# The two float32r parts of a stationary weight in one buffer, element by element, in a decoder trunk on one Trainium2 core

## Chip, cores and metric

One core of one Trainium2 chip runs the whole program in a single launch. The metric is the device time of that launch in microseconds (us). Three runs of the kernel before gave 2358.15, 2359.06 and 2359.34 us; the median, 2359.06 us, is what the change is held against.

## What is computed

Two layers of a decoder trunk on x of 512 tokens by 1024 channels, in float32, and a last RMSNorm. Each layer has two sub-layers:

```
h = rmsnorm(x, norm1_w)
(z, xbc, dt, gq, gk, gv, g_lr, g_r, qkv, gates) = split(h @ w_in)       # 1024 -> 12320 columns
y_ssd, y_gla, y_att = state space, gated linear attention, dilated window attention
merged = sum_i sigmoid(gates_i) * (y_i @ w_branch_i)
x = x + merged @ w_out
h = rmsnorm(x, norm2_w)
gate, val = split(h @ ffn_up)                                           # 1024 -> 2 x 2816
x = x + (silu(causal_conv3(gate)) * val) @ ffn_down
```

Nearly all of the arithmetic is in the products with w_in, w_branch, w_out, ffn_up and ffn_down.

## The kernel before

**How a product is made.** Each float32 operand is split in two float32r parts, a high part h and a rest lo, so that h + lo is the value. A product is then three matmuls into the same PSUM bank (`mm3`): high with high, high with rest, rest with high. The activations of a layer lie in eight pairs of tiles `xh`, `xl` of 128 channels by 512 tokens, written once per norm. The weights come in units of 128 x 1024 values. There are 374 of them, in the order of `weight_plan`, and each takes 24 matmuls of 512 columns.

**A weight unit.** `unit` (it takes unit u) calls `fetch(u + 6)`, which issues the transfer of a unit from HBM into one of four `raw` buffers on SyncE's queue, and `parts(u + 3)`, which splits a unit: ScalarE copies `raw` into the float32r tile `wh` (line 248) and VectorE subtracts that from `raw` into `wl` (line 250). The pool `wgt` has three buffers of each.

**Two kinds of unit.** In a unit "cm" (`proj_cm`, `branch` and the down projection; 318 units) the weights are stationary: TensorE loads 128 columns of `wh` or `wl` and streams 512 columns of an activation pair past them. The activation is `xh`/`xl` in 226 units (113 a layer) and a pair from the pool `big` in 92: `ya`, `yg`, `ys` (branch outputs), `mg` (merged), `hh`/`hl` (hidden layer of the MLP). In a unit "tm" (`proj_tm`; 56 units) it is the other way round: 128 columns of `xh` or `xl` are loaded, and 512 columns of `wh` or `wl` stream. In 40 of these the loaded columns lie side by side (`blk`), in 16 they are read with a step of four elements (`res`).

**Order of work.** TensorE runs its matmuls in the order in which the code records them. The large matmuls of a unit wait in a queue, `large`; the small float32 matmuls of the side work (scores, scans, transposes) are recorded between units, and each is followed by one large matmul (line 182; the others are on line 177). The instructions of VectorE and ScalarE are ordered by the framework's scheduler.

**Where buffers lie.** Pools are laid out in the order in which they are opened. In the built program `xh` and `xl` (pool `cp`) fill bytes 30688 to 63455 of each partition, `wh` and `wl` bytes 86720 to 111295, `big` bytes 111296 to 217791. 30688 is 32 more than a multiple of 64; 86720 and 111296 are multiples of 64, and every tile of these pools is a multiple of 2048 bytes long, so that all of a pool's tiles share that remainder. `own_c`, a small stationary operand of the state space branch, starts at 28128, which also is 32 more than a multiple of 64.

Of the kernel before, what the change touches and what calls it, by code (L numbers as in the profile page):

```python
# [12 lines left out]
F32R = mybir.dt.float32r  # L13
# [5 lines left out]
PSUM = bass.MemoryType.PSUM  # L19

P = 128
T = 512
D = 1024
KD = D // P
# [7 lines left out]

# columns of the packed per-channel parameters
O_N1, O_N2, O_SCW, O_SCB, O_SNW, O_GB, O_GNW, O_FCW, O_FCB, N_PC = (
    0, 8, 16, 80, 96, 104, 106, 107, 173, 195)


# The order of the work between the projections of the linear attention and the gates of the state
# space branch: z (two groups), x/B/C of a group, two output blocks of the other branches.
MIX = ([("att", m) for m in (0, 2, 4, 6)] + [("z", 0), ("xbc", 0), ("xbc", 1), ("gla", 0), ("z", 1), ("xbc", 2)]  # L40
# [3 lines left out]
def weight_plan(depth):  # L44
    """The order in which the kernel takes its weight units (128 x 1024 values each)."""
    plan = []
    for l in range(depth):
# [23 lines left out]
        for kind, n in MIX:  # L71
# [5 lines left out]
            else:  # L77
                i, row = (2, 12) if kind == "att" else (1, 8)
# [18 lines left out]
def shape_constants():  # L97
    """Arrays that depend on the shapes alone."""
    f = np.float32
# [37 lines left out]
def hybrid_decoder(ctx: ExitStack, tc: tile.TileContext, ins, out):  # L137
    nc = tc.nc
    depth = ins["pc"].shape[0]
    plan = weight_plan(depth)  # L140
# [3 lines left out]
    def nm(s):  # L144
        ids[0] += 1
        return f"{s}_{ids[0]}"

    cp = ctx.enter_context(tc.tile_pool(name="cp", bufs=1))
    lp = ctx.enter_context(tc.tile_pool(name="lp", bufs=1))
    raw_p = ctx.enter_context(tc.tile_pool(name="raw", bufs=4))  # L150
    wgt_p = ctx.enter_context(tc.tile_pool(name="wgt", bufs=3))
    big_p = ctx.enter_context(tc.tile_pool(name="big", bufs=52))
    sml_p = ctx.enter_context(tc.tile_pool(name="sml", bufs=20))
# [15 lines left out]

    # The large matmuls of a weight unit wait in a queue, and each small one of the side work is  # L170
    # followed by one of them: a small one's stationary operand then loads behind a large one.
    large = deque()
# [26 lines left out]

    # ---- side work: generators that are stepped between weight units; each yields the number of  # L200
    # units after which the operands of its next step are there ----
    sides = []
# [31 lines left out]

# [1 line left out]
    raws, units = [], []  # L236
# [7 lines left out]
    def parts(n):  # L244
        while len(units) < min(n, len(plan)):
            r = raws[len(units)]
            h = wgt_p.tile([P, 1024], F32R, tag="wh", name=nm("wh"))
            A.copy(h, r)  # L248
            lo = wgt_p.tile([P, 1024], F32R, tag="wl", name=nm("wl"))
            V.tensor_sub(lo, r, f(h))  # L250
            units.append((h, lo))
# [39 lines left out]

# [1 line left out]
    mats = cp.tile([P, 3, P], F32, name="mats")  # L293
# [5 lines left out]
    pcs, rows, gws = [], [], []  # L299
# [24 lines left out]

    xh = [cp.tile([P, T], F32R, name=f"xh{m}") for m in range(KD)]
    xl = [cp.tile([P, T], F32R, name=f"xl{m}") for m in range(KD)]
    xhl = list(zip(xh, xl))
    rstdB = cp.tile([P, T], F32, name="rstdB")
# [15 lines left out]

# [1 line left out]
    def split(h, lo, src, w):  # L346
        """h + lo = src * w"""
        A.activation(h, src, AF.Copy, scale=w)  # L348
        V.scalar_tensor_tensor(lo, src, w, f(h), ALU.mult, ALU.subtract)
# [12 lines left out]
    def norm_stats(acc, both):  # L362
        """rstdB, and the factors of the tokens in block (and residue) order"""
        n = 8 if both else 4
        ss = mx()
        for c in range(n):
            mm(ss[:, c:c + 1], acc[:, blk(c) if c < 4 else res(c - 4)], ones[:, 0:1], True, True)
        return factors(ss, n)
# [18 lines left out]

# [1 line left out]
    def attention(yh, yl, pre):  # L389
# [36 lines left out]
    def attention_head(h, vt, qk, yh, yl):  # L426
        hc = blk(h)
        # scores, masked, with their row maxima: [0] block order, [1] residue order
        st = [sml([P, 2, 4], n="st") for _ in range(2)]
        pr = []  # L430
        for d in range(2):
            for half in range(2):
                s = mx()
                for j in range(2):
                    n = 2 * half + j
                    if d == 0:
                        lo = 0 if n else P
# [6 lines left out]
                p = big([P, 2, 256], n="pr")  # L444
                for j in range(2):
                    n = 2 * half + j
                    lo = P if (d == 0 and n == 0) else 0
# [3 lines left out]
        for d in range(2):  # L451
            nb = sml([P, 4], n="nb")
            V.tensor_scalar(nb, st[d][:, 0], -ATT_C, None, ALU.mult)
            for n in range(4):
                lo = P if (d == 0 and n == 0) else 0
                p = pr[2 * d + n // 2][:, n % 2, lo:]
                A.activation(p, p, AF.Exp, bias=nb[:, n:n + 1], scale=ATT_C, accum_out=st[d][:, 1, n:n + 1])
        # the groups' weights: exp(m - M) / sum, computed in residue order
        ex = sml([P, 4, 2, 4], n="ex")
# [34 lines left out]
        for d in range(2):  # L494
            for n in range(4):
                lo = P if (d == 0 and n == 0) else 0
# [3 lines left out]
        yield 1  # L500
        # transposes; block-order columns go to (residue, index) order
        pt = []
# [29 lines left out]

# [1 line left out]
    def small_proj():  # L534
# [5 lines left out]

# [1 line left out]
    def gla_decay(l, gd, las):  # L542
# [147 lines left out]

# [1 line left out]
    def ssd_decay(l, gd, dec):  # L692
# [14 lines left out]
        A.activation(u, u, AF.Exp)  # L707
        # log1p(u) = 2 atanh(z), z = u / (2 + u) <= 1/3
        rd = sml([P, n], n="rd")
# [25 lines left out]
        V.tensor_mul(dte, dt, e[:, 1])  # L735
        # the cumulative sums as rows (twice): the upper copy is replaced by the rest of the split
        ac2 = big([P, 2, 64], n="ac2")
# [16 lines left out]
    def conv_silu(o, width, w, b, dst):  # L754
        """dst = 2 w-conv of (o * rstd), then v (tanh v + 1): w and b are halved"""
        x = big([P, T], n="cx")
        V.tensor_mul(x, o, rstdB)  # L757
        v = big([P, T], n="cv")
        A.activation(v, x, AF.Identity, bias=b, scale=w(width - 1))
        for i in range(1, width):  # L760
            V.scalar_tensor_tensor(v[:, i:], x[:, :T - i], w(width - 1 - i), v[:, i:], ALU.mult, ALU.add)  # L761

        def end():
            A.activation(x, v, AF.Tanh)  # L764
            V.scalar_tensor_tensor(dst, x, 1.0, v, ALU.add, ALU.mult)

        return end
# [25 lines left out]
    def ssd_group(l, g, dec, ch, zw, yh, yl):  # L793
# [10 lines left out]

        # token-major x and B
        xdt, xd, xe = [], [], []
# [91 lines left out]

# [1 line left out]
    def gate():  # L900
# [41 lines left out]

# [1 line left out]
    def new_acc():  # L944
# [18 lines left out]
    for l in range(depth):  # L963
# [76 lines left out]
        if not end:  # L1040
            side(norm_side(acc, True), 2)
# [1 line left out]
    sq = big([P, T], n="sq")  # L1043
# [16 lines left out]
def lay_out(inputs):  # L1060
    """The program's arrays: the inputs, rearranged only."""
    a = {k: np.asarray(v) for k, v in inputs.items()}
# [54 lines left out]
```

## Time and profile before

| | us |
|---|---|
| median of three runs | 2359.06 |
| span of the profiled execution | 2355.0 |
| difference, outside the span | 4.1 |
| TensorE matmul busy (10776 instructions) | 2332.6 (99%) |
| TensorE weight load busy | 1921.1 (82%) |
| VectorE busy | 1413.3 (60%) |
| ScalarE busy | 902.9 (38%) |
| DMA queue 1, share of 16 engines | 27.9% |

How to read it: the profile is of one execution, whose span is 4.1 us under the median of the runs; what a step saves of the span it saves of the median. Matmuls are pipelined, so that a record of a matmul is longer than the time from its start to the next one's start; it is the latter that adds up to the span, and the timeline's start times give it. A weight load (PEld) runs beside the matmul before it. "Idle before" is time in which an engine waited, with the instruction that ended the wait.

### The profile page before, as it was taken

Reading aid. Unit: us, or ns where it says so; the run is one execution under the profiler, and the core shown is the slowest. Engines: PE = TensorE matmul, PEld = TensorE weight load, DVE = VectorE, ACT = ScalarE, POOL = GpSimd, SP = SyncE. Lnnn points to the kernel's source line nnn. Section 1 sums busy time; section 2 is a strip of 40 time slices with the busy share of each in tenths; the row PEclk is TensorE's granted clock in tenths of the full one; section 3 lists DMA queues with packets and bytes.
Section 4 is the critical chain, followed back from the end, with each engine's and each line's share of the span. In section 5 each row is a group of like instructions: output and inputs, shape, how many; then the busy total and the mean of one; then the engine's idle time right before and its main releaser. Section 6 shows DMA issues by size and latency. Waiting matters only on the chain.

```text
span 2355.0 us, 27385 instructions
## 1 busy us (share of the span) xinstructions
PE 2332.6 (99%) x10776; PEld 1921.1 (82%) x10776; DVE 1413.3 (60%) x2511; ACT 902.9 (38%) x1487; POOL 0.2 (0%) x4
## 2 busy tenths in 40 slices
PE   8999999999999999999999999999999999999997
PEld 7888878888888888888898888788888888888886
DVE  4467548687865565553425764676888556555533
ACT  4344423444443333332224444234454433333321
POOL 0000000000000000000000000000000000000000
PEclk9999999999999999999999999999999999999998
DMA  5322222222222323233323222222222232333231
GB/s 180 99 81 78 75 63 90 79 65 72 81 81 90 99 90 99 90 99 94 95 89 99 81 81 70 73 82 72 72 74 79 81 99 90 99 90 99 91 98 54
DMA packets 58512, 204.21 MB, mean 87 GB/s; under 512 B 7152, under 2 KB 7824, under 8 KB 58384
## 3 DMA queue, kind: packets, MB, share of 16 engines
q1 hardware_dynamic: 57808, 201.42, 27.9%
q8 instruction: 84, 1.38, 0.2%
q10 hardware_dynamic: 576, 1.05, 0.1%
q14 instruction: 44, 0.36, 0.0%
HBM read 200.35 MB, written 2.10 MB: 86 GB/s over the span
## 4 chain that ended last, share of the span: by engine, by line
PE 98%; DVE 1%; ACT 0%; DMA 0%; issue 0%; DVEq 0%; SPq 0%; ACTq 0%
PE pp L177 78%; PE pp L182 11%; PE mx L185 8%; PE mx L189 1%; DVE x L1055 0%; DVE wl L250 0%; DMA x<-in_xT 0%; ACT wh L248 0%; DVE th L904 0%; DVE th L929 0%; DVE cv L761 0%; ACT L348 0%; ACT cx L764 0%; ACT th L905 0%; DVE M L882 0%
## 5 line engine op out<-in xcount | busy, mean ns | idle before, releaser
L248 ACT CAST wh<-raw 128x1024 fp32r<-128x1024 f32 x374 | 392.3, 1049 | 992.1 <-PE pp L177 764.0
L250 DVE TENSOR_TENSOR wl<-raw,wh 128x1024 fp32r<-128x1024 f32 x374 | 457.7, 1224 | 374.5 <-ACT wh L248 368.9
L177 PE MATMUL pp<-xh,wl 128*128 128x512 f32 x1582 | 625.2, 395 | 0.0
L177 PE MATMUL pp<-xl,wh 128*128 128x512 f32 x1556 | 614.9, 395 | 0.0
L177 PE MATMUL pp<-xh,wh 128*128 128x512 f32 x1504 | 595.0, 396 | 0.0
L177 PEld LDWEIGHTS pp<-xh,wl 128*128 128x128 f32 x1582 | 297.0, 188 | 72.1 <-issue 1.0
L177 PEld LDWEIGHTS pp<-xl,wh 128*128 128x128 f32 x1556 | 292.3, 188 | 68.9 <-issue 0.5
L177 PEld LDWEIGHTS pp<-xh,wh 128*128 128x128 f32 x1504 | 282.4, 188 | 68.8 <-DVE wl L250 1.5
L177 PE MATMUL pp<-wh,xl 128*128 128x512 f32 x392 | 156.1, 398 | 0.0
L177 PE MATMUL pp<-wh,xh 128*128 128x512 f32 x372 | 148.4, 399 | 7.3 <-ACT wh L248 7.3
L177 PE MATMUL pp<-wl,xh 128*128 128x512 f32 x386 | 154.6, 401 | 0.5 <-DVE wl L250 0.5
L182 PE MATMUL pp<-xh,wh 128*128 128x512 f32 x304 | 148.1, 487 | 0.0
L177 PE MATMUL pp<-hh,wh 128*128 128x512 f32 x352 | 137.1, 390 | 0.0
L177 PE MATMUL pp<-hh,wl 128*128 128x512 f32 x352 | 137.1, 390 | 0.0
L177 PE MATMUL pp<-hl,wh 128*128 128x512 f32 x352 | 137.1, 389 | 0.0
L757 DVE TENSOR_TENSOR cx<-pp,rstdB 128x512 f32<-128x512 f32 x76 | 52.4, 689 | 129.7 <-PE pp L177 129.6
L182 PE MATMUL pp<-xl,wh 128*128 128x512 f32 x252 | 124.4, 494 | 0.0
L182 PE MATMUL pp<-xh,wl 128*128 128x512 f32 x226 | 110.4, 489 | 0.0
L764 ACT ACTIVATE cx<-cv 128x512 f32<-128x512 f32 x76 | 48.1, 632 | 138.7 <-DVE cv L761 138.2
L177 PEld LDWEIGHTS pp<-wh,xh 128*128 128x128 f32 x372 | 86.2, 232 | 18.3 <-ACT wh L248 7.3
L177 PEld LDWEIGHTS pp<-wh,xl 128*128 128x128 f32 x392 | 89.9, 229 | 11.7
L177 PEld LDWEIGHTS pp<-wl,xh 128*128 128x128 f32 x386 | 88.8, 230 | 12.5 <-DVE wl L250 1.0
(267 smaller groups left out, 3389.4 us busy)
## 6 DMA issues: line engine op xcount, KB each, us to landing
raw<-in_wall SPq DMA_DIRECT2D x374, 512.0 KB, 3.6
x<-in_xT SPq DMA_DIRECT2D x8, 256.0 KB, 5.9
out_dram<-x ACTq DMA_DIRECT2D x4, 256.0 KB, 2.3
out_dram<-x SPq DMA_DIRECT2D x4, 256.0 KB, 2.5
cosR<-in_rope SPq DMA_DIRECT2D x2, 256.0 KB, 3.9
sinR<-in_rope SPq DMA_DIRECT2D x2, 256.0 KB, 4.7
amask<-in_amask SPq DMA_DIRECT2D x1, 256.0 KB, 5.3
levf<-in_lev SPq DMA_DIRECT2D x1, 224.0 KB, 3.6
```

Of the source, the lines that this page charges most:

```text
L177: PE.matmul(o, lhsT=l, rhs=r, start=start, stop=stop)
L182: PE.matmul(o, lhsT=l, rhs=r, start=start, stop=stop)
L185: PE.matmul(o, lhsT=l, rhs=r, start=start, stop=stop)
L189: PE.transpose(o, i, idn)
L248: A.copy(h, r)
L250: V.tensor_sub(lo, r, f(h))
L757: V.tensor_mul(x, o, rstdB)
L764: A.activation(x, v, AF.Tanh)
```

## The change

`wh` and `wl` of a unit become one tile `w` of 2048 elements. In a unit "cm" the high part takes the even elements and the rest the odd ones, so that the load of 128 stationary columns reads every second element. In a unit "tm" the two parts lie one behind the other and stream as before. ScalarE's copy and VectorE's subtraction write, and VectorE reads the high part, with a step of two in units "cm". Two pools are opened in another order, and `xh`, `xl` get a pool of their own (the diff's lines that only drop comments are left out):

```diff
     cp = ctx.enter_context(tc.tile_pool(name="cp", bufs=1))
     lp = ctx.enter_context(tc.tile_pool(name="lp", bufs=1))
+    xp = ctx.enter_context(tc.tile_pool(name="xp", bufs=1))
     raw_p = ctx.enter_context(tc.tile_pool(name="raw", bufs=4))
+    big_p = ctx.enter_context(tc.tile_pool(name="big", bufs=52))
     wgt_p = ctx.enter_context(tc.tile_pool(name="wgt", bufs=3))
-    big_p = ctx.enter_context(tc.tile_pool(name="big", bufs=52))
...
             r = raws[len(units)]
-            h = wgt_p.tile([P, 1024], F32R, tag="wh", name=nm("wh"))
+            w = wgt_p.tile([P, 2048], F32R, tag="w", name=nm("w"))
+            if plan[len(units)][0] == "tm":
+                h, lo = w[:, :1024], w[:, 1024:]
+            else:
+                wv = w.rearrange("p (n two) -> p two n", two=2)
+                h, lo = wv[:, 0], wv[:, 1]
             A.copy(h, r)
-            lo = wgt_p.tile([P, 1024], F32R, tag="wl", name=nm("wl"))
             V.tensor_sub(lo, r, f(h))
             units.append((h, lo))
...
-    xh = [cp.tile([P, T], F32R, name=f"xh{m}") for m in range(KD)]
-    xl = [cp.tile([P, T], F32R, name=f"xl{m}") for m in range(KD)]
+    xh = [xp.tile([P, T], F32R, name=f"xh{m}") for m in range(KD)]
+    xl = [xp.tile([P, T], F32R, name=f"xl{m}") for m in range(KD)]
```

In the built program of the change `xh` and `xl` fill bytes 37568 to 70335, `big` bytes 86720 to 193215 and `w` bytes 193216 to 217791; 37568 and 193216 are multiples of 64, as 86720 is. `own_c` stays where it was. The number and the order of TensorE's matmuls and of SyncE's transfers are the same; the scheduler moves the split of a unit on ScalarE and VectorE, as follows.

ScalarE, in the projections of the first attention head of layer 0 (`sw` are the halves of a rotated product, copied out of PSUM `pp`; `raw`, `wh` and `w` belong to the split). Before:

```order
L248 CAST wh_658<-raw_551 128x1024
L248 CAST wh_697<-raw_581 128x1024
L413 COPY sw_686<-pp_655 64x512
L414 COPY sw_686<-pp_655 64x512
L248 CAST wh_736<-raw_611 128x1024
L413 COPY sw_725<-pp_694 64x512
L414 COPY sw_725<-pp_694 64x512
```

And with the change:

```order
L254 CAST w_647<-raw_543 128x1024
L418 COPY sw_674<-pp_644 64x512
L419 COPY sw_674<-pp_644 64x512
L254 CAST w_685<-raw_572 128x1024
L418 COPY sw_712<-pp_682 64x512
L419 COPY sw_712<-pp_682 64x512
L254 CAST w_723<-raw_601 128x1024
```

The copy of a unit's high part stood ahead of the two copies out of PSUM of the same step; now it stands behind them.

VectorE at the same place (`ra`, `sw` and `qk` are the rotation of a product). Before:

```order
L250 TENSOR_TENSOR wl_699<-raw_581,wh_697 128x1024
L416 TENSOR_TENSOR ra_689<-pp_655,cosR_649 128x512
L417 TENSOR_TENSOR sw_686<-sw_686,sinR_650 128x512
L422 TENSOR_TENSOR qk_692<-ra_689,sw_686 128x512
L250 TENSOR_TENSOR wl_738<-raw_611,wh_736 128x1024
L416 TENSOR_TENSOR ra_728<-pp_694,cosR_649 128x512
```

And with the change:

```order
L421 TENSOR_TENSOR ra_677<-pp_644,cosR_638 128x512
L422 TENSOR_TENSOR sw_674<-sw_674,sinR_639 128x512
L255 TENSOR_TENSOR w_685<-raw_572,w_685 128x1024
L427 TENSOR_TENSOR qk_680<-ra_677,sw_674 128x512
L421 TENSOR_TENSOR ra_715<-pp_682,cosR_638 128x512
L422 TENSOR_TENSOR sw_712<-sw_712,sinR_639 128x512
```

The subtraction stood ahead of the rotation of the same step; now it stands behind the rotation's first two instructions.

## Rows read from the trace of the kernel before

**Rows 1.** The page: busy time of the engines, and the granted TensorE clock in 40 slices of the span (tenths; 9 is 90% or more).

```profile
PE 2332.6 (99%) x10776; PEld 1921.1 (82%) x10776; DVE 1413.3 (60%) x2511; ACT 902.9 (38%) x1487; POOL 0.2 (0%) x4
...
PEclk9999999999999999999999999999999999999998
```

**Rows 2.** The page: the chain of work that ended last, shares of the span by engine and by line.

```profile
PE 98%; DVE 1%; ACT 0%; DMA 0%; issue 0%; DVEq 0%; SPq 0%; ACTq 0%
PE pp L177 78%; PE pp L182 11%; PE mx L185 8%; PE mx L189 1%; DVE x L1055 0%; DVE wl L250 0%; DMA x<-in_xT 0%; ACT wh L248 0%; DVE th L904 0%; DVE th L929 0%; DVE cv L761 0%; ACT L348 0%; ACT cx L764 0%; ACT th L905 0%; DVE M L882 0%
```

**Rows 3.** TensorE's waits on the split: who waited for whom, us in total, how often, the longest.

```profile
PE pp L177 <- ACT wh L248: 7.3, 1, 7.3
...
PE pp L177 <- DVE wl L250: 0.5, 1, 0.5
```

**Rows 4.** Groups of TensorE's matmuls by line and shape: out<-moving,stationary, partitions x columns, count | busy us, mean ns of one record | idle before.

```profile
L177 PE MATMUL pp<-xh,wl 128*128 128x512 f32 x1582 | 625.2, 395 | 0.0
...
L177 PE MATMUL pp<-wh,xl 128*128 128x512 f32 x392 | 156.1, 398 | 0.0
...
L182 PE MATMUL pp<-xh,wh 128*128 128x512 f32 x304 | 148.1, 487 | 0.0
L177 PE MATMUL pp<-hh,wh 128*128 128x512 f32 x352 | 137.1, 390 | 0.0
...
L177 PE MATMUL pp<-ysh,wh 128*128 128x512 f32 x128 | 49.9, 390 | 0.0
...
L177 PE MATMUL pp<-mgh,wh 128*128 128x512 f32 x128 | 49.8, 389 | 0.0
...
L177 PE MATMUL pp<-yah,wl 128*128 128x512 f32 x56 | 21.9, 391 | 0.0
...
L185 PE MATMUL mx<-qsb,ksb 128*128 128x128 f32 x224 | 42.9, 273 | 0.0
...
L185 PE MATMUL mx<-xg,own_c 128*128 128x512 f32 x32 | 12.6, 395 | 0.0
...
L185 PE MATMUL mx<-qsb,ksb 128*128 128x512 f32 x16 | 8.2, 591 | 0.0
```

**Rows 5.** Groups of TensorE's weight loads, same columns.

```profile
L177 PEld LDWEIGHTS pp<-xh,wl 128*128 128x128 f32 x1582 | 297.0, 188 | 72.1 <-issue 1.0
...
L177 PEld LDWEIGHTS pp<-hl,wh 128*128 128x128 f32 x352 | 66.1, 188 | 13.6
```

**Rows 6.** Timeline of TensorE in the up projection of the MLP of layer 0 (units "cm", moving `xh`/`xl`): start us, duration us, engine, line. First and last of 26 matmuls in a row.

```profile
902.78 0.40 PE L177 MATMUL pp<-xl,wh 128*128 128x512 f32 x1
...
908.61 0.39 PE L177 MATMUL pp<-xh,wl 128*128 128x512 f32 x1
```

**Rows 7.** The same in the down projection of layer 0 (units "cm", moving `hh`/`hl`): first and last of 26.

```profile
1099.80 0.39 PE L177 MATMUL pp<-hh,wl 128*128 128x512 f32 x1
...
1105.46 0.39 PE L177 MATMUL pp<-hh,wh 128*128 128x512 f32 x1
```

**Rows 8.** The same in a unit "tm" whose stationary columns lie side by side: first and last of 27, and one load.

```profile
19.66 0.40 PE L177 MATMUL pp<-wh,xh 128*128 128x512 f32 x1
...
19.89 0.19 PEld L177 LDWEIGHTS pp<-wh,xl 128*128 128x128 f32 x1
...
25.73 0.40 PE L177 MATMUL pp<-wh,xl 128*128 128x512 f32 x1
```

**Rows 9.** The same in a unit "tm" whose stationary columns are read with a step of four elements: first and last of 28, and one load.

```profile
39.42 0.40 PE L177 MATMUL pp<-wh,xl 128*128 128x512 f32 x1
...
40.14 0.31 PEld L177 LDWEIGHTS pp<-wh,xh 128*128 128x128 f32 x1
...
45.84 0.40 PE L177 MATMUL pp<-wh,xl 128*128 128x512 f32 x1
```

**Rows 10.** Groups of ScalarE and VectorE. The outputs of lines 530 and 531 are written with a step of four elements; those of lines 248, 250, 1014 and 416 without a step.

```profile
L248 ACT CAST wh<-raw 128x1024 fp32r<-128x1024 f32 x374 | 392.3, 1049 | 992.1 <-PE pp L177 764.0 <-issue 201.6 <-PE pp L182 20.4
...
L1014 ACT CAST hh<-fs 128x512 fp32r<-128x512 f32 x44 | 27.3, 621 | 4.3 <-DVE fs L1012 4.2
...
L530 ACT CAST yah<-mx 128x512 fp32r<-128x512 f32 x8 | 8.6, 1079 | 40.8 <-PE mx L185 40.8
...
L250 DVE TENSOR_TENSOR wl<-raw,wh 128x1024 fp32r<-128x1024 f32 x374 | 457.7, 1224 | 374.5 <-ACT wh L248 368.9 <-PE mx L185 4.0
...
L416 DVE TENSOR_TENSOR ra<-pp,cosR 128x512 f32<-128x512 f32 x48 | 33.1, 689 | 17.1 <-ACT sw L414 17.1
...
L531 DVE TENSOR_TENSOR yal<-mx,yah 128x512 fp32r<-128x512 f32 x8 | 8.7, 1093 | 36.5 <-ACT yah L530 36.5
```

**Rows 11.** Timeline of ScalarE and VectorE over a step of the rotated projections of layer 0 (the place of the order rows above).

```profile
86.59 1.05 ACT L248 CAST wh<-raw 128x1024 fp32r<-128x1024 f32 x1 [3.74 <-PE pp L177]
87.66 0.58 ACT L413 COPY sw<-pp 64x512 f32<-64x512 f32 x1
88.26 0.58 ACT L414 COPY sw<-pp 64x512 f32<-64x512 f32 x1
92.19 1.05 ACT L248 CAST wh<-raw 128x1024 fp32r<-128x1024 f32 x1 [3.35 <-PE pp L177]
...
87.67 1.23 DVE L250 TENSOR_TENSOR wl<-raw,wh 128x1024 fp32r<-128x1024 f32 x1 [2.36 <-ACT wh L248]
```

**Rows 12.** Busy time of the engines in the densest stretch of the side work: start and end us, length, then busy us and instructions of each engine, granted clock, DMA share, GB/s.

```profile
472.00:531.00 59.00, 58.31 (x312) 48.51 (x311) 50.72 (x114) 27.62 (x69) 0.00 (x0) 1.00 0.21 63
```

## Prediction

> **What bounds the kernel now.** I read the page first: TensorE's matmuls are busy 99% of the span, and the granted clock is at its upper level, 2.4 GHz, throughout [rows 1]. Then the chain of work that ended last: 98% of it is TensorE, 89% the large float32r matmuls of lines 177 and 182 [rows 2]. Then TensorE's waits: on the split of a weight unit it waited twice, 7.8 us together [rows 3], and both waits lie at the program's start. So the time is a sum of start-to-start steps of matmuls, and the change counts by what it does to one step. The timeline gives these steps:
>
> - moving `xh`/`xl`, stationary weight: (908.61 - 902.78) / 25 = 233.2 ns [rows 6]
> - moving `hh`/`hl`, stationary weight: (1105.46 - 1099.80) / 25 = 226.4 ns [rows 7]
> - moving weight, stationary `xh`/`xl` side by side: (25.73 - 19.66) / 26 = 233.5 ns [rows 8]
> - moving weight, stationary `xh`/`xl` with a step of four: (45.84 - 39.42) / 27 = 237.8 ns [rows 9]
>
> All four stream 512 columns, which at 2.4 GHz is 213.3 ns, so each step has 13 to 25 ns on top. The load itself (188 ns as recorded, [rows 5]) is shorter than a step and runs beside the matmul before it, so its length does not show. Two things seem to make the excess. First, whatever touches `xh`/`xl` is slower by 7 ns, in either role: records of `ys`, `mg`, `ya` and `hh` as moving operands are 389 to 391 ns, `ya` in the same stage as `xh` ones, against 395 ns [rows 4]. Those four come from a pool whose tiles start at a multiple of 64 bytes; `xh`, `xl` start 32 bytes off one. The one other large float32r operand that does so, `own_c`, is also in a 395 ns record [rows 4]. Second, 13.1 ns remain where both operands are at a multiple of 64. The float32 matmuls, whose columns take two cycles, show none of it: (591 - 273) / (512 - 128) = 0.828 ns a column [rows 4] against 0.833 ns for two cycles. So the excess appears only where the moving operand is read at full rate; I read it as the load's reads getting in the way of the stream's.
>
> **The change part by part.**
>
> *The place of `xh`, `xl`.* They move from 32 bytes off a multiple of 64 to a multiple of 64. I take it that the 7 ns go. 226 units "cm" times 24 matmuls are 5424, at 233.2 - 226.4 = 6.8 ns: 36.9 us. 56 units "tm" times 24 are 1344, at 233.5 - 226.4 = 7.1 ns: 9.5 us. Together **-46.4 us**. Bounds: nothing, if it is the region of memory and not the remainder that makes `xh` slow. The matmuls of line 182, 11% of the chain against 78% on line 177 [rows 2], are followed by a small one; if they kept their step the gain would be an eighth less, 6 us.
>
> *The load with a step of two.* 318 units "cm" times 24 are 7632 matmuls whose load now reads 1024 bytes for 128 columns instead of 512. The trace has no step of two. Its neighbours are a step of one and of four [rows 8, 9]: with four the recorded load grows from 190 to 310 ns, still beside the stream, and the step by 237.8 - 233.5 = 4.3 ns. That bounds a loss at 7632 x 4.3 = 33 us, unless two differs in kind from both. A gain is bounded by the whole excess, 7632 x 13.1 = 100 us. I take **0**: with four, 24.5 ns of excess lie on a load that reads 16 bytes a column; half the span of memory at half of that excess is 12 ns, next to the 13.1 ns of a step of one. On this the Trainium skill speaks twice (SBUF — State Buffer, Door 1, the note on cachelines): two hits in a 16-byte line suffice for full bandwidth, which a step of two 4-byte elements just has, and a step of four has not; the longer load of the latter agrees with it. By that sentence too this term is 0.
>
> *The split writes with a step of two* in 318 units. Nearest rows are the writes with a step of four, which also read PSUM: 1079 against 621 ns for 512 elements on ScalarE, 1093 against 689 on VectorE [rows 10], or 0.9 and 0.8 ns an element. For 1024 elements that is at most 0.9 and 0.8 us more for each split; the other end is nothing. ScalarE would go from 903 to 1190 us and VectorE from 1413 to 1670, both under the span: **0** while they are covered. Cover is thinnest where VectorE has 50.72 of 59 us [rows 12]; some nine units there would add 7 us and just fill it. Beyond that the side work would be late, a few us per layer.
>
> *The split moves behind the copies and half the rotation.* The copy to the high part starts two copies later, 1.16 us, and the subtraction ends about as much later than at 88.90 [rows 11]. A step of this stage is 92.19 - 86.59 = 5.60 us. The split fills the buffer that the unit just ended gave back, and is needed two units on, 11.2 us after; it took 2.3 us and now takes 3.5 to 5.2. **0**, covered by 6 us. Behind it on VectorE waits `qk`, whose head's scores come units later. `raw` is given back 1.2 us later, and its transfer is issued that much later on SyncE's queue; four buffers in 5.6 us steps cover that.
>
> *One buffer for both parts.* It is given back after the last matmul of the unit, one matmul (0.23 us) later than the high part was: **0**, by the same cover.
>
> Sum: 2359.1 - 46.4 = **2313 us**. It is made on the profiled execution (span 2355.0), 4.1 us under the median; that difference I leave as it is.
>
> **Rivals.**
>
> *The step of two ends the conflict.* With a step of two the load advances by 8 bytes a column, the stream by 4. If a load takes columns at half the stream's rate, the two then go through memory at one pace, and two readers at one pace, once out of each other's way, stay so. The Trainium skill (TensorE: Matmul & The Clock Gate, LDWEIGHTS) gives a load as its columns over 1.2 GHz, which is that half; no row here shows a load's rate alone. For it: in the float32 matmuls stream and load (of a step of one) also go at one pace, and there the excess is nil [rows 4]. Against it: these also leave half of the memory's time free, which explains the same row. It would take up to 13.1 ns from 7632 matmuls, down to 2313 - 100 = 2213 us; I let it stand for 2213 to 2250.
>
> *Each line costs.* If the 13.1 ns are the price of the 32 pieces of 16 bytes that a load takes from the stream, a step of two takes 64 and costs 13.1 ns more: 2313 + 100 = 2413 us. It decides above 46.4 us / 7632 = 6.1 ns a matmul. Against it: with a step of four, 128 pieces, the step grew by 4.3 ns only. The same note of the Trainium skill has this too: each access that crosses to a new line pays.
>
> *As with a step of four.* +4.3 ns on 7632 matmuls gives 2346 us.
>
> *The place does nothing.* If `xh` is slow for its region (it stays under byte 70336) and the step of two is neutral, the time stays at 2359 us.
>
> **How the numbers follow.** A difference under 0.2%, 4.7 us, can't be told from none. The forecast (2300 to 2326) gets 0.36: two classes of operands separate cleanly, and one remainder separates them. The end of the conflict (2213 to 2250) gets 0.24, something between it and the forecast 0.08, a loss like a step of four (2326 to 2350) 0.13, no change 0.08, slower by lines 0.11. Faster is 0.36 + 0.24 + 0.08 + 0.13 = 0.81, same 0.08, slower 0.11. A range from 2215 to 2350 leaves out the last two, 0.19. The forecast's own range is 2300 to 2326.
>
> **What would show it.** In the up projection the step from matmul to matmul falls from 233.2 to 226 ns, in the down projection it stays at 226, in the first units "tm" it falls from 233.5 to 226. Down projection at 214 to 218: the conflict has ended. Down projection above 231, and recorded loads well above 188 ns: the step of two costs. Up projection and the units "tm" at 233 still: the remainder of 64 is not the cause. Waits of TensorE on the split past the start would mean that the cover is gone. The forecast is wrong if the time leaves 2300 to 2326.

## The result, and the profile after

The changed kernel takes 2373.72 us (median of four runs, 2373.10 to 2373.89), the kernel before on the same chip 2359.20 us (four runs, 2358.15 to 2362.25). The ratio is 1.0061 with a 95% interval of 1.0049 to 1.0073: **slower by 0.6%**, where 2% faster was forecast, and outside the range. The span grew from 2355.0 to 2371.8 us, by 16.8 us where the medians are 14.5 apart. The profiled execution of the kernel before is one of its quickest: runs with a span of 2355.0 us took 2356.74 and 2356.80 us, so 1.8 us lies outside the span, and the other 2.3 of the 4.1 us are the spread of its executions. That spread goes with the granted clock (2356.74 us at a mean of 0.997, 2362.64 us at 0.995).

The page of the kernel after, in the parts that answer to [rows 1, 2, 5, 10]; the columns are the same.

```profile
PE 2348.4 (99%) x10776; PEld 1963.7 (83%) x10776; DVE 1408.6 (59%) x2511; ACT 923.4 (39%) x1487; POOL 0.2 (0%) x4
...
PEclk9999999999999999999999999999999999999998
...
PE 98%; DVE 1%; ACT 0%; DMA 0%; issue 0%; DVEq 0%; SPq 0%; ACTq 0%
...
L254 ACT CAST w<-raw 128x1024 fp32r<-128x1024 f32 x374 | 418.1, 1118 | 899.2 <-PE pp L178 701.5
L178 PEld LDWEIGHTS pp<-xh,w 128*128 128x128 f32 x3086 | 598.0, 194 | 124.2 <-issue 2.4
L255 DVE TENSOR_TENSOR w<-raw,w 128x1024 fp32r<-128x1024 f32 x374 | 457.8, 1224 | 376.7 <-ACT w L254 376.3
```

Nothing has changed in what bounds the kernel: TensorE fills 98% of the chain, at the upper clock level but for 3.4 us near 1505 us (a granted clock of 0.66 over 1504 to 1509 us), whose nine matmuls take 1.5 us more than before. The load with a step of two is recorded 6 ns longer (194 for 188 ns). The split costs VectorE nothing and ScalarE 69 ns more on the mean. TensorE's waits, which answer to [rows 3] (us in total, times, longest):

```profile
PE pp L178 <- ACT w L254: 8.1, 1, 8.1
...
PE pp L178 <- DVE w L255: 0.5, 1, 0.5
```

The two waits are still those at the start. So, as before, the time is the sum of start-to-start steps, and the steps of the named places tell what happened. TensorE in the up projection (as [rows 6]), where consecutive matmuls of the same operands now share a row ("x2"). Each weight gives three matmuls, one of which moves `xl`, so three steps lie between two `xl` rows:

```profile
902.89 0.39 PE L178 MATMUL pp<-xl,w 128*128 128x512 f32 x1
...
908.49 0.39 PE L178 MATMUL pp<-xl,w 128*128 128x512 f32 x1
```

In the down projection (as [rows 7]):

```profile
1121.29 0.39 PE L178 MATMUL pp<-hl,w 128*128 128x512 f32 x1
...
1126.19 0.39 PE L178 MATMUL pp<-hl,w 128*128 128x512 f32 x1
```

In a unit "tm" with stationary columns side by side (as [rows 8]):

```profile
20.25 0.39 PE L178 MATMUL pp<-w,xl 128*128 128x512 f32 x1
...
25.70 0.39 PE L178 MATMUL pp<-w,xl 128*128 128x512 f32 x1
```

| place | step before, ns | step after, ns |
|---|---|---|
| up projection, moving `xh`/`xl` | 233.2 | (908.49 - 902.89) / 24 = 233.3 |
| down projection, moving `hh`/`hl` | 226.4 | (1126.19 - 1121.29) / 21 = 233.3 |
| unit "tm", side by side | 233.5 | (25.70 - 20.25) / 24 = 227.1 |

The rows give starts to 0.01 us, so that a step over 21 to 27 matmuls is good to some 0.4 ns. By the trace's own nanoseconds the down projection before and the unit "tm" after are both at 226.7.

The units "tm" fell as forecast; in them nothing is loaded with the new step. The up projection, most of the forecast gain, did not move. The down projection, which was to stay, lost 6.7 ns a step. Since the 10776 matmuls come in the same order in every kernel here that keeps the units, the steps can be added up by kind over the whole trace. The ledger below is worked out from the start times of all matmuls of the profiled executions ("small" are the float32 matmuls of the side work; a step belongs to the matmul it begins with). e1 is the first experiment below, the change without the step of two.

| step | count | before, us | after - before | of this, e1 - before | after - e1 |
|---|---|---|---|---|---|
| "cm" moving `xh`/`xl`, a large one next | 4636 | 1093.5 | +3.0 | -25.3 | +28.4 |
| the same, a small one next | 788 | 249.0 | +4.5 | +0.2 | +4.3 |
| "cm" moving a pair of `big`, a large one next | 2141 | 487.1 | +13.8 | -0.1 | +14.0 |
| the same, a small one next | 67 | 19.9 | +0.4 | 0 | +0.4 |
| "tm", a large one next | 1150 | 275.0 | -5.0 | -4.8 | -0.2 |

With the start of the first matmul 0.7 us later (8.05 for 7.32) and 1 us less after small matmuls, this is the 16.8 us of the span within 0.2. The last two columns are the answer in short: the place gave 30 us, the step of two took 47 (by the medians of the runs 33 and 47: 2359.50, 2326.31 and 2373.72 us).

### The profile page after: what moved, and what is told of

The parts are those of the page before. It is cut to its first block, busy times and chain, and to the rows that moved or that the text cites. A ratio compares the mean times of both kernels' runs of the same rounds, so it can differ in the third digit from the quotient of the medians.

```text
span 2371.8 us, 27415 instructions
## 1 busy us (share of the span) xinstructions
PE 2348.4 (99%) x10776; PEld 1963.7 (83%) x10776; DVE 1408.6 (59%) x2511; ACT 923.4 (39%) x1487; POOL 0.2 (0%) x4
## 3 DMA queue, kind: packets, MB, share of 16 engines
q10 hardware_dynamic: 576, 1.05, 0.1%
## 4 chain that ended last, share of the span: by engine, by line
PE 98%; DVE 1%; ACT 0%; DMA 0%; issue 0%; DVEq 0%; SPq 0%; ACTq 0%
PE pp L178 78%; PE pp L183 11%; PE mx L186 8%; PE mx L190 1%; DVE x L1060 0%; DMA x<-in_xT 0%; DVE w L255 0%; ACT w L254 0%; DVE th L909 0%; DVE th L934 0%; DVE cv L766 0%; ACT th L910 0%; ACT L353 0%; ACT cx L769 0%; DVE M L887 0%
## 5 line engine op out<-in xcount | busy, mean ns | idle before, releaser
L178 PE MATMUL pp<-xh,w 128*128 128x512 f32 x3086 | 981.1, 395 | 0.0
L254 ACT CAST w<-raw 128x1024 fp32r<-128x1024 f32 x374 | 418.1, 1118 | 899.2 <-PE pp L178 701.5
L178 PEld LDWEIGHTS pp<-xh,w 128*128 128x128 f32 x3086 | 598.0, 194 | 124.2 <-issue 2.4
L255 DVE TENSOR_TENSOR w<-raw,w 128x1024 fp32r<-128x1024 f32 x374 | 457.8, 1224 | 376.7 <-ACT w L254 376.3
L178 PE MATMUL pp<-xl,w 128*128 128x512 f32 x1556 | 614.1, 395 | 0.0
L178 PEld LDWEIGHTS pp<-xl,w 128*128 128x128 f32 x1556 | 301.6, 194 | 60.5 <-issue 0.5
L183 PE MATMUL pp<-xh,w 128*128 128x512 f32 x530 | 251.1, 494 | 0.0
L178 PE MATMUL pp<-w,xh 128*128 128x512 f32 x758 | 238.9, 395 | 8.5 <-ACT w L254 8.1
L178 PE MATMUL pp<-hh,w 128*128 128x512 f32 x704 | 221.4, 394 | 0.0
L178 PEld LDWEIGHTS pp<-w,xh 128*128 128x128 f32 x758 | 164.9, 230 | 29.2 <-ACT w L254 8.0
L178 PE MATMUL pp<-w,xl 128*128 128x512 f32 x392 | 154.5, 394 | 0.0
L183 PE MATMUL pp<-xl,w 128*128 128x512 f32 x252 | 125.7, 499 | 0.0
L183 PEld LDWEIGHTS pp<-xh,w 128*128 128x128 f32 x530 | 104.2, 197 | 17.6 <-issue 1.4
```

Source lines behind the costliest of these rows:

```text
L178: PE.matmul(o, lhsT=l, rhs=r, start=start, stop=stop)
L183: PE.matmul(o, lhsT=l, rhs=r, start=start, stop=stop)
```

## Experiments

All ratios are to the kernel before on the same chip, with 95% intervals; each was timed in several rounds unless said otherwise. In the expectations a theory goes by a letter: S, the load with a step of two costs; S', it costs, but not on top of a bad place; L, each line of memory that a load touches costs; R, it is the region of memory that makes `xh` slow; D, it is the difference between the places of the two operands; D256 (and the like), that difference taken as a multiple of so many bytes.

### The place alone

```diff
-            if plan[len(units)][0] == "tm":
-                h, lo = w[:, :1024], w[:, 1024:]
-            else:
-                wv = w.rearrange("p (n two) -> p two n", two=2)
-                h, lo = wv[:, 0], wv[:, 1]
+            h, lo = w[:, :1024], w[:, 1024:]
```

> The change's pools and its one buffer, but in all units the rest lies behind the high part, so that every load reads side by side; the order of the splits is the change's. Theory S (the step of two costs 6.9 ns a matmul, the place of xh and xl gives 6.8): steps of 226.4 ns in up projection, down projection and units tm alike, 2313 us. Rival R (the new region of the weights, byte 193216 on, costs the 7 ns of the down projection, and the step of two nothing): down projection stays at 233, up projection at 233, 2372 to 2376 us.

Measured: 2326.31 us, ratio 0.9854 (0.9840 to 0.9869). TensorE of this kernel in the up projection and in the down projection:

```profile
903.39 0.39 PE L178 MATMUL pp<-xl,w 128*128 128x512 f32 x1
...
908.15 0.39 PE L178 MATMUL pp<-xl,w 128*128 128x512 f32 x1
...
1120.99 0.39 PE L178 MATMUL pp<-hl,w 128*128 128x512 f32 x1
...
1126.43 0.39 PE L178 MATMUL pp<-hl,w 128*128 128x512 f32 x1
```

That is (908.15 - 903.39) / 21 = 226.7 ns in the up projection and (1126.43 - 1120.99) / 24 = 226.7 ns in the down projection. So the place does what the forecast said of it to a step, `xh` still lies under byte 70336, so that R falls, and the step of two is what costs. It is the load that costs, not the split's writes with that step: more than 24 matmuls behind a small one, nine in ten of the change's `xh`/`xl` steps are at 233 or 234 ns, though the split is written in only some 2.4 of each 5.6 us. The gain is 30 us of span, not 46.4. The steps tell why: sorted by how far back the last small matmul lies, the steps of `xh`/`xl` units fall from 233.3 to 226.7 ns more than 24 matmuls behind it (2728 of them) and from 233.3 to 227.4 at 7 to 24 (1292), but from 233.1 only to 232.4 at 3 to 6 (408). Part of that last is the clock: it was at its lower level for 3.4 us of this execution (a granted clock of 0.76 over 1475 to 1482 us), and without the steps in that stretch the mean at 3 to 6 is 230.5. The first two behind a small one gain nothing. S holds in the steps; its time, 2313 us, was 13 us too low.

### The step of two alone

The pools as before (`xh`, `xl` in `cp`, `wgt` before `big`), and the change's interleaved `w`.

```diff
-    xp = ctx.enter_context(tc.tile_pool(name="xp", bufs=1))
-    big_p = ctx.enter_context(tc.tile_pool(name="big", bufs=52))
     wgt_p = ctx.enter_context(tc.tile_pool(name="wgt", bufs=3))
+    big_p = ctx.enter_context(tc.tile_pool(name="big", bufs=52))
...
-    xh = [xp.tile([P, T], F32R, name=f"xh{m}") for m in range(KD)]
+    xh = [cp.tile([P, T], F32R, name=f"xh{m}") for m in range(KD)]
```

> Pools as before, xh and xl 32 bytes off a multiple of 64, weights interleaved as in the change. Theory S, the two costs adding: up projection 240, down projection 233.3, units tm 233.5 ns, 2359 + 7632 x 6.9 ns = 2412 us. Theory S', the two costs not adding (either one brings a step to 233): up projection 233, down projection 233.3, units tm 233.5, 2359 + 2208 x 6.9 ns = 2374 us. Rival R (region): as before, 2359 us.

Measured: 2380.75 us, ratio 1.0087 (1.0072 to 1.0102). TensorE in the up projection of this kernel:

```profile
903.00 0.40 PE L177 MATMUL pp<-xl,w 128*128 128x512 f32 x1
...
908.60 0.40 PE L177 MATMUL pp<-xl,w 128*128 128x512 f32 x1
...
1121.40 0.39 PE L177 MATMUL pp<-hl,w 128*128 128x512 f32 x1
...
1126.30 0.39 PE L177 MATMUL pp<-hl,w 128*128 128x512 f32 x1
```

(908.60 - 903.00) / 24 = 233.3 ns, as with the bad place alone (233.2) and with the step of two alone (233.3, after); the down projection, in the last two rows, is at (1126.30 - 1121.40) / 21 = 233.3. **The two do not add**: S' holds in the long runs of large matmuls. The median is 7 us above S' (2374). Of the 26.1 us by which the span of the profiled execution grew, 14.3 lie in the steps that move a pair of `big`, as S' has it (15.2), and 4.7 in the `xh`/`xl` steps before a small matmul, where S' has nothing and the change has 4.5. A further 5.6 lie in the `xh`/`xl` steps before a large one, but 3.9 of these are the clock's. It was at its lower level for 6.8 and 3.4 us of this execution, and not in the same work before. Here are a row of this kernel in the first of those stretches and one of the kernel before around the same work (columns as in [rows 12]; the granted clock is the third number from the end):

```profile
336.00:342.00 6.00, 6.00 (x15) 4.44 (x15) 0.43 (x2) 0.00 (x0) 0.00 (x0) 0.50 0.00 0
...
328.00:338.00 10.00, 10.00 (x38) 6.22 (x38) 3.71 (x10) 1.14 (x2) 0.00 (x0) 1.00 0.18 53
```

### A step of four

Two blocks of 128 columns share a piece of the buffer, high, rest, high, rest; so the load reads every fourth element.

```diff
-                wv = w.rearrange("p (n two) -> p two n", two=2)
-                h, lo = wv[:, 0], wv[:, 1]
-            A.copy(h, r)
-            V.tensor_sub(lo, r, f(h))
+                wv = w.rearrange("p (b n f) -> p b f n", n=P, f=4)
+                rv = r.rearrange("p (b i n) -> p b i n", i=2, n=P)
+                hv, lv = wv[:, :, bass.ds(0, 2, step=2)], wv[:, :, bass.ds(1, 2, step=2)]
+                A.copy(hv, rv)
+                V.tensor_sub(lv, rv, f(hv))
+                h, lo = Blocks(hv, 2), Blocks(lv, 2)
```

> The change's pools; in units cm two neighbouring blocks of 128 columns share a piece, high, rest, high, rest, so that a load reads every fourth element. Theory S (as the units tm with a step of four in the changed kernel, 235 ns against 226.7 side by side): 235 ns, 1.9 more than with a step of two, 2374 + 7632 x 1.9 ns = 2388 us. Rival L (the cost goes with the 16-byte pieces a load touches: 32 side by side, 64 with a step of two, 128 with four): 233.3 + 13.8 = 247 ns, 2374 + 105 = 2479 us. Rival R: 2374 us.

Measured: 2506.54 us, ratio 1.0615 (1.0597 to 1.0632); both expectations missed the time. The groups of this kernel (one load, the large matmuls that a small one follows, the split):

```profile
L189 PEld LDWEIGHTS pp<-xh,w 128*128 128x128 f32 x3086 | 848.8, 311 | 4.0 <-issue 1.5
...
L194 PE MATMUL pp<-xh,w 128*128 128x512 f32 x530 | 307.8, 601 | 0.0
...
L268 ACT CAST w<-raw 128x1024 fp32r<-128x1024 f32 x318 | 655.5, 2063 | 553.2 <-PE pp L189 350.6 <-issue 158.6 <-PE pp L194 28.2
...
L269 DVE TENSOR_TENSOR w<-raw,w 128x1024 fp32r<-128x1024 f32 x318 | 651.0, 2047 | 388.5 <-ACT w L268 387.9
```

And TensorE in its up projection:

```profile
902.97 0.39 PE L189 MATMUL pp<-xl,w 128*128 128x512 f32 x1
...
908.61 0.39 PE L189 MATMUL pp<-xl,w 128*128 128x512 f32 x1
```

Between large matmuls the step is (908.61 - 902.97) / 24 = 235.0 ns, only 1.7 ns more than with a step of two: there S holds, and L, whose price doubles with the lines, falls. Most of the loss is beside the small matmuls: the record of line 194 is 601 ns where the change has 494, and by the ledger the 788 `xh`/`xl` steps before a small matmul take 439 ns on the mean where the kernel before has 316, 97 of the 153 us by which the span grew. In the median they take 432 for 315 ns. That is 117 ns more, about as much as the load grew (188 to 311 ns), so I take it that a small matmul of 128 columns is too short a cover for such a load; no run tests this by itself.

Two other things are in that loss. TensorE now waits for the side work, whose engines take about twice as long over a split as before:

```profile
PE mx L201 <- DVE pr L519: 10.2, 6, 2.0
...
PE mx L201 <- ACT sy L911: 4.4, 2, 2.2
```

The kernel before has neither wait; the eight steps that hold these are 16.6 of the 97 us. And the clock was at its lower level in ten stretches, 61 us together, ahead of the one at the end that every kernel here has. The longest were at 352 and 1591 us:

```profile
352.00:362.00 10.00, 10.00 (x23) 6.00 (x23) 4.58 (x13) 0.00 (x0) 0.00 (x0) 0.50 0.17 52
1591.00:1604.00 13.00, 13.00 (x29) 8.20 (x29) 5.05 (x13) 0.00 (x0) 0.00 (x0) 0.50 0.14 40
```

The 158 matmuls in the ten stretches took 66.7 us, the same ones before 36.9: up to 30 of the 153 us come with the clock.

### High with high, rest with rest

Is it that high and rest share pieces of memory, or the step as such? Here blocks of the high part are interleaved two by two, and blocks of the rest likewise; the step is two.

```diff
-                wv = w.rearrange("p (n two) -> p two n", two=2)
-                h, lo = wv[:, 0], wv[:, 1]
+                rv = r.rearrange("p (b i n) -> p b i n", i=2, n=P)
+                hv, lv = (t.rearrange("p (b n i) -> p b i n", i=2, n=P) for t in (h, lo))
```

> The change's pools and its step of two in units cm, but two blocks of the high part lie side by side element by element, and two of the rest; no load reads high and rest from the same piece of memory. Theory S (the step costs): steps of 233.3 ns in up and down projection, 2374 us. Rival H (what costs is that high and rest share their pieces): 226.5 ns, 2326 us.

Measured: 2373.66 us, ratio 1.0061 (1.0046 to 1.0076), the time of the change. TensorE in its down projection:

```profile
1121.00 0.39 PE L189 MATMUL pp<-hl,w 128*128 128x512 f32 x1
...
1126.60 0.39 PE L189 MATMUL pp<-hl,w 128*128 128x512 f32 x1
```

233.3 ns again: H falls. It is the step, whatever lies between.

### Which place: is it the multiple of 64?

Three kernels move the operands of e1. The tiles of `xh`, `xl` get 16 elements more, so that they lie 2112 bytes apart and their starts differ from tile to tile by multiples of 64; they are used from byte 32, 16 or 64 on. In the first the weights are 32 bytes off too, and their three buffers lie 8256 bytes apart.

```diff
-    xh = [xp.tile([P, T], F32R, name=f"xh{m}") for m in range(KD)]
+    xh = [xp.tile([P, T + 16], F32R, name=f"xh{m}")[:, 8:8 + T] for m in range(KD)]
...
-            w = wgt_p.tile([P, 2048], F32R, tag="w", name=nm("w"))
+            w = wgt_p.tile([P, 2064], F32R, tag="w", name=nm("w"))[:, 8:8 + 2048]
```

That is the first; the other two have `[:, 4:4 + T]` and `[:, 16:16 + T]` and leave `w` as it was.

> As e1_place_only, no step, but xh, xl and the weights all start 32 bytes off a multiple of 64; the pool big stays at multiples. Theory A (each operand for itself wants a multiple of 64): 233 ns in up projection, down projection and units tm, 2326 + 25 + 5 + 14 = 2370 us. Rival D (the difference of the two operands counts): up projection and units tm at 226.5, down projection at 233 ns, 2326 + 14 = 2340 us.

> As e1_place_only, but xh and xl start 16 bytes off a multiple of 64. Theory A64 (any remainder of 64 costs): up projection and units tm at 233 ns, down projection at 226.5, 2326 + 30 = 2356 us. Rival A32 (16 bytes stay within half of 64 and cost nothing): 226.5 ns everywhere, 2326 us.

> As e1_place_only, but xh and xl start 64 bytes further on, at multiples of 64 whose remainders of 128 differ from tile to tile. Theory A64: 226.5 ns everywhere, 2326 us. Rival A128 (a larger power of two counts): up projection partly at 233 ns, up to 2356 us.

Measured: 2366.80 us, ratio 1.0027 (1.0016 to 1.0038); 2353.61 us, 0.9974 (0.9964 to 0.9984); 2350.85 us, 0.9967 (0.9955 to 0.9979). The first two are near theory A's times (2370 and 2356); in the first, D's 233 ns for the down projection came, its 226.5 for the up projection did not ((908.66 - 903.11) / 24 = 231.3): there the differences are 0, 64, 128 or 192 (modulo 256), from tile to tile and buffer to buffer. In the third all starts are multiples of 64, and its up projection still is slow, as A128 had it (the first two rows; the others are the down projection of the first kernel):

```profile
902.87 0.39 PE L178 MATMUL pp<-xl,w 128*128 128x512 f32 x1
...
908.66 0.39 PE L178 MATMUL pp<-xh,w 128*128 128x512 f32 x1
...
1121.18 0.39 PE L178 MATMUL pp<-hl,w 128*128 128x512 f32 x1
...
1126.08 0.40 PE L178 MATMUL pp<-hl,w 128*128 128x512 f32 x1
```

25 steps of 231.6 ns. **The multiple of 64, on which the forecast built its first term, falls.** In the first the down projection, whose `hh` moved by 1024 bytes only (16 tiles ahead of it grew by 64), rose to 233.3 ns (21 steps in the rows, single ones of 229 to 238) when the weights moved by 32 bytes. So the place of neither operand decides alone.

### The difference of the two starts

The kernel before with 288 bytes of padding ahead of `raw`:

```diff
     lp = ctx.enter_context(tc.tile_pool(name="lp", bufs=1))
+    lp.tile([P, 72], F32, name="pad")
     raw_p = ctx.enter_context(tc.tile_pool(name="raw", bufs=4))
```

`xh` stays at 30688, the weights move to 87008 and `big` to 111584: all start 32 bytes off a multiple of 64, and all differ by multiples of 512.

> The kernel before with one pad of 288 bytes between xh, xl and the weights, nothing else. All large operands then have the same remainder of 512, and all start 32 bytes off a multiple of 64. Theory D (what counts is the difference of the starts of stream and load, which is a multiple of 512 now): 226.5 ns in up projection, down projection and units tm, 2326 us or a little less. Rival A (each operand wants a multiple of 64 for itself): 233 ns everywhere, 2360 + 14 = 2374 us.

Measured: 2324.92 us, ratio 0.9853 (0.9837 to 0.9870). TensorE in the up projection:

```profile
902.83 0.39 PE L178 MATMUL pp<-xh,wh 128*128 128x512 f32 x1
...
908.72 0.39 PE L178 MATMUL pp<-xh,wl 128*128 128x512 f32 x1
```

26 steps of 226.5 ns, with every operand off the multiple of 64: D holds, and A falls. Before, it was 288 bytes (modulo 512) between `xh` and the weights; with the change 0. To see of which number it has to be a multiple, e1 got a gap between `xh`, `xl` and the pools behind them, so that only their difference changes:

```diff
     xp = ctx.enter_context(tc.tile_pool(name="xp", bufs=1))
+    gap_p = ctx.enter_context(tc.tile_pool(name="gap", bufs=1))
+    gap_p.tile([P, 64], F32, name="gap")
```

This is the gap of 256 bytes; 32 and 16 elements make the 128 and 64 bytes.

> As e1_place_only with a gap of 256 bytes behind xh and xl, so that stream and load of xh, xl against weights differ by 256 of 512 throughout; all starts at multiples of 64. Theory D with 512: up projection 230 to 233 ns, 2340 to 2356 us. Rival D256 (a difference of a multiple of 256 is enough): 226.5 ns, 2326 us.

> As f6_diff_256 with a gap of 128 bytes: stream and load of xh, xl against weights differ by 128 of 256 throughout. Theory D256 (the difference must be a multiple of 256): up projection and units tm at 231 to 234 ns, 2346 to 2358 us. Rival D128: 226.5 ns, 2326 us.

> As f6_diff_256 with a gap of 64 bytes: a difference of 64 throughout. Theory D256: up projection and units tm at 231 to 234 ns, 2346 to 2358 us. Rival D64 (the remainder of 64, as the prediction had it, where only constant differences count): 226.5 ns, 2326 us.

| difference, bytes | time, us | ratio | up projection, ns |
|---|---|---|---|
| 256 | 2326.74 | 0.9861 (0.9846 to 0.9876) | 226.8 |
| 128 | 2355.24 | 0.9986 (0.9976 to 0.9995) | 232.1 |
| 64 | 2361.56 | 1.0009 (1.0000 to 1.0019) | 233.3 |

Their rows, in the order of the table (25, 24 and 24 steps):

```profile
903.03 0.39 PE L180 MATMUL pp<-xl,w 128*128 128x512 f32 x1
...
908.70 0.39 PE L180 MATMUL pp<-xh,w 128*128 128x512 f32 x1
```

```profile
903.06 0.39 PE L180 MATMUL pp<-xl,w 128*128 128x512 f32 x1
...
908.63 0.40 PE L180 MATMUL pp<-xl,w 128*128 128x512 f32 x1
```

```profile
903.01 0.40 PE L180 MATMUL pp<-xl,w 128*128 128x512 f32 x1
...
908.61 0.40 PE L180 MATMUL pp<-xl,w 128*128 128x512 f32 x1
```

In these three the down projection keeps its 226.5 to 226.7 ns, as `hh` and the weights moved together. D with 512, D128 and D64 fall; the last kernel's time is 4 us above the range that D256 gave it, its step within. Where all tiles share one difference, of those tried only a multiple of 256 bytes gives the fast step: modulo 256, 0 is fast, and 32 (the kernel before), 64 and 128 are not. At 128 the single steps run from 228 to 241 ns, at 64 they alternate between 230 and 236. Pair by pair the rule is not shown. In the third kernel of the section before, tiles 3 and 7 of `xh` and of `xl` lie a multiple of 256 from the weights; the steps that begin with them (more than 24 matmuls behind a small one) average 230.0 ns where the other tiles have 231.7 to 232.8, and not 226.7. The padded kernel and e1 cannot be told apart (their intervals overlap) and beat both the kernel before and the change; the padding is one line.

### A step of eight

As the step of four, with four blocks sharing (`f=8`, `i=4`); timed in two runs.

> As e3_step_four, but four neighbouring blocks share a piece, so that a load reads every eighth element. Theory L (from a step of four on each column lies in a 16-byte piece of its own, and the load costs by pieces): as with a step of four, loads of 310 ns, 2506 us. Rival B (the load costs by the bytes it spans): 235 ns becomes 240 or more, loads longer than 310 ns, above 2600 us.

Measured: 2578.62 us, ratio 1.0929 (1.0907 to 1.0951); L fell. B held in the step and the load, not in the time. The load, and TensorE in the up projection:

```profile
L189 PEld LDWEIGHTS pp<-xh,w 128*128 128x128 f32 x3086 | 893.6, 329 | 3.7 <-issue 1.5
```

```profile
902.75 0.40 PE L189 MATMUL pp<-xl,w 128*128 128x512 f32 x1
...
905.68 0.41 PE L189 MATMUL pp<-xl,w 128*128 128x512 f32 x1
```

The load grows from 311 to 329 ns, the step from 235.0 to (905.68 - 902.75) / 12 = 244.2 ns. Over steps of one, two, four and eight elements the matmul's step is 226.7, 233.3, 235.0 and 244.2 ns: neither a fixed price nor one by the line.

## Why the prediction was wrong

**The step that failed** is "*The load with a step of two* ... I take **0**". It costs 6.1 ns on 4636 matmuls, 5.4 on 788 and 6.5 on 2141, 47 us in all (the change against e1). The bound beside it (33 us) failed for the same reason: it came from a step of four against one of one, 4.3 ns [rows 8, 9], and both rows stand at a place where the step of one already paid 7 ns for the difference of starts. The step-only kernel shows that these prices do not add. With the place mended the same comparison gives 7.9 ns: 227.1 against 235.0 ns in the units "tm" of the kernel after, whose rows with a step of four are

```profile
39.23 0.40 PE L178 MATMUL pp<-w,xl 128*128 128x512 f32 x1
...
45.81 0.40 PE L178 MATMUL pp<-w,xh 128*128 128x512 f32 x1
```

(6.58 us over 28 steps.) The rows that could have warned are those of the down projection [rows 7]: a pair that already ran at 226.4 ns had 7 ns to lose, and the prediction itself had called it the only class without that excess, yet priced its loss from rows that had it. Of the two signs that the prediction named for a step of two that costs, one came, the down projection above 231 ns; the recorded load stayed at 194.

The Trainium skill (SBUF — State Buffer, Door 1, the note on cachelines) says that two hits in a 16-byte line suffice for full bandwidth. The load's own record agrees: 188 and 194 ns at steps of one and two, 311 at four, 329 at eight. The time does not: the matmuls under which that load runs are 6.7 ns a step longer already at two. The measurement decides. The note's other sentence, that each crossing to a new line pays, has the right sign here, but not as a price for each line, since four costs only 1.7 ns more than two.

**"The place of xh, xl"** was right in sign and, far from small matmuls, in size (233.3 to 226.7 ns where 6.8 ns were forecast), wrong in its count and its cause. Some 4020 of 5424 steps "cm" gained, about 6.4 ns each, and the units "tm" 4.8 us for 9.5; 30 us for 46.4. The prediction had the reserve of an eighth for matmuls followed by a small one, but not for the several that come after it. It also gave all 56 units "tm" the same 7.1 ns; in the 16 that are read with a step of four the step fell by only 2.8 (237.8 [rows 9] to 235.0). In place of the remainder of 64 the runs showed the difference between the starts modulo 256, which sorted the rows of before just as well as the multiple of 64: `big` and the weights differed by 0, `xh` and the weights by 32 (modulo 256).

**The split** was right in all three terms. No wait of TensorE came beyond the two at the start; here the step of the rotated projections that [rows 11] show before, ScalarE's and VectorE's rows of after:

```profile
87.44 0.58 ACT L419 COPY sw<-pp 64x512 f32<-64x512 f32 x1
88.05 1.13 ACT L254 CAST w<-raw 128x1024 fp32r<-128x1024 f32 x1
...
89.26 1.22 DVE L255 TENSOR_TENSOR w<-raw,w 128x1024 fp32r<-128x1024 f32 x1
```

The split ends at 90.48 where it ended at 88.90, 1.6 us later, under a cover of 6 us. The padded kernel and e1 say the same: they have the same step of one and fast places, the first with the old order and two buffers, the second with the new order and one, and their times (2324.92 and 2326.31 us) cannot be told apart. The bound of 0.9 us for writes was far too wide: ScalarE's copy went from 1.05 to 1.13 us, VectorE's subtraction stayed at 1.22.

**The rivals.** "Each line costs" came out in its direction, with half its price (6.6 for 13.1 ns) and, by the step of four, not by its mechanism; its point of decision, 6.1 ns, was passed narrowly, and with a gain of 30 in place of 46.4 that was enough. "The step of two ends the conflict" is refuted: 13 ns over 213.3 remain in every kernel here. "As with a step of four" had the right thought, a loss of the load, but its price from the masked rows. "The place does nothing" is refuted by e1.

**Open:** why it is a multiple of 256 and why tiles with mixed differences do not follow it one by one; why a load with a step of two slows the matmul above it while its own record hardly grows; why matmuls near small ones gain little or nothing; what the last 13 ns are; and why the clock falls where it does. No experiment here bears on them.

## What to carry to other kernels

When the step between matmuls that cover a load has an excess, look up the start addresses of the moving and the stationary operand in the built program, and pad one so that they differ by a multiple of 256 bytes in all tiles: 1.5% here for one line. Price an edit from rows that are in the state the edit will meet; an excess that is already there can hide the one that is added. Two edits in one change should be run apart: here one was worth about -30 us and the other +47. Before a small difference between two profiles is put down to the edit, compare their granted clocks stretch by stretch: 1.5 to 4.5 us of a span came with it here, and up to 30 with the step of four.

## What the runs showed of the hardware

- A large float32r matmul whose covered load reads side by side takes 226.5 to 226.8 ns a step when stream and load start a multiple of 256 bytes apart throughout (0 and 256 tried), and 231 to 233.5 ns on the mean at the other differences tried (32, 64 and 128 modulo 256 throughout, and mixed ones).
- The same load with a step of two 4-byte elements has a record of 194 for 188 ns, but the matmul above it takes 233.3 ns a step, with either place.
- Writing with a step of two 4-byte elements cost VectorE nothing (1224 ns for 1024) and ScalarE 0.08 us; with four it was 2047 and 2063 ns, about double.
- A load with a step of four shows little under large matmuls (+1.7 ns over a step of two) and much beside short float32 ones (the step before one takes 432 ns in the median where a step of one has 315 and a step of two 323).
